# Six score buffers, ten activation items ahead of the gates, and four or five scatters per item by turns

## The chip, the cores and the metric

The kernel runs on one core of a Trainium2 chip. The metric is the device time of one execution in microseconds (us). The engines are named as in the profile: PE (matrix multiplications), PEld (its weight loads), DVE (vector), ACT (scalar), POOL (GpSimd), SP (the queue that issues most transfers). All engines run side by side, each through its own list of instructions in a fixed order.

## What is computed

One layer of a streaming encoder on 512 tokens (and 16 meta tokens) of width 2048: a mixer of 16 attention heads, then a channel mixer ("PEER") that picks 8 x 16 of 16384 single-neuron experts for each token. The change touches the second part only. Cut to that:

```
def block(hb):                                   # 128 tokens
    q = (hb @ w_query).reshape(128, 8, 2, 128)
    s = einsum('thpc,hpnc->thpn', q, sub_keys)   # 2 x 128 scores per head
    top_s, top_i = top_k(s, 16)
    cand_s = top_s[:, :, 0, :, None] + top_s[:, :, 1, None, :]
    cand_i = top_i[:, :, 0, :, None] * 128 + top_i[:, :, 1, None, :]
    best_s, best_j = top_k(cand_s, 16)           # over the 256 pairs of a head
    idx = take_along_axis(cand_i, best_j)
    g = softmax(best_s)
    a = gelu(einsum('thkd,td->thk', u[idx], hb))
    return einsum('thk,thkd->td', g * a, v[idx])
```

## The kernel before

The attention and the output projection fill the first 1030 us or so of the profile. The expert part has these stages.

**Queries and top-k.** For each of 16 query blocks (8 heads, two halves) `project` (line 199) multiplies a block of `w_q` with the tokens: 48 matmuls of 128x512, since each float32 product is made of three. A weight half arrives in `wr`; ACT casts quarters of it into `wh` (line 183), and DVE or POOL makes the remainder `wl` (line 184). `score` (lines 789 to 801) makes the scores of a block on PE into PSUM tile `zs`, and ACT copies them with a scale into `sc` (line 795), one of three buffers of [128, 4, 128] floats. After each second block `topk` (lines 737 to 787) puts some 70 instructions on DVE; the first reads and the match-and-replace steps of it use the two `sc` tiles of the head. The `sc` buffer of block c is free for block c+3 once line 750 of its head is done.

**Items.** The dense part treats tokens 128 to 511 against all experts in 128 chunks of 128 experts. Chunk j is an item: a block of `uT` is cut into `wh` and `wl`, 48 matmuls of 128x384 make its activations in PSUM tile `pa`, and ACT applies GELU into `ga` (line 873). For most items `ga` goes to DRAM (`a_scr`). The first `NAP` items after number `JC` (16) are made by `project` (line 212 on PE, `wl` on POOL); the others, called A(j), in the list `items` by `mm_u` (line 994 on PE, `wl` on DVE). Items 16 to 19 are of the first kind before, and A(20) is the first of the second; its `wl` too is made on POOL. At t = `GATES` = 1 of the list `gates` is called (lines 878 to 891): the exponential and the softmax over the chosen scores, the expert numbers `idx0`, and the scatter addresses `dst`. It needs the whole of `topk`. The list's DVE work is written out in order: the cut of A(21), then `gates`, then the cut of A(22).

**Work beside the items.** Two kinds of work are laid between the `wl` cuts of each A item after that. `due(WA)` hands out gathered rows for the first 128 tokens: `fetch` (line 828) is an indirect gather of 1 MB on POOL into one of three buffers `gr`, two rows ahead of `consume` (lines 843 and 846, two DVE instructions a row). It gives out 256 rows over A, D and V items. `scatter` (lines 910 to 932) has one step per call: line 914 sums the gates of one choice on DVE into one column of `tot`, and line 926 writes such a column into `g_scr` in DRAM, an indirect scatter of 128 single floats on POOL. There are 384 of each. `NSC` steps are given to each A or D item. PE, DVE, ACT and SP keep the order in which the list is written; POOL's order is chosen by the scheduler, which puts each scatter right behind its own sum rather than a head later.

**The rest.** After the A items come 16 D items, which read `g_scr` (`load_gates`, three items ahead), then eight rounds of V items, in which PE multiplies gated activations with rows of `v` (line 1016).

The order of the items is two lines, the first of which the change moves through `NAP`:

```
items = [("A", j) for j in range(JC + NAP, P)] + [("D", j) for j in range(JC)]
work = due(WA) + [sc] * NSC
```

Of the kernel before, what the change touches and what calls it, by code (L numbers as in the profile page):

```python
# [9 lines left out]
F32 = mybir.dt.float32  # L10
# [7 lines left out]
PSUM = bass.MemoryType.PSUM  # L18
DRAM = bass.MemoryType.DRAM

P = 128
# [3 lines left out]
D = 2048  # L25
KD = D // P
NH = 8
NTB = T // P
# [5 lines left out]
EPS = 1e-6  # L34
NEG = -1e30
H = D // 2
NAP = 4
GATES = 1
WA = 2.1
JC = 16  # L40
LEAD = JC // 2 + 1
NSC = 6
AHEAD = 3


class Lanes:
    """Steps of generators, run between pieces of the tensor engine's main stream.

    A generator yields (pieces to wait, next step uses the shared bank)."""

    def __init__(self):
        self.q = {}
# [39 lines left out]
def hymba_peer(ctx: ExitStack, tc: tile.TileContext, xT, w_in, w_fl, b_fg, g_mix, g_q, g_k, g_merge,  # L92
# [16 lines left out]

    nc.scalar.preload_act_table_set("natural_log_exp_and_others")  # L110

# [1 line left out]
    ident = cst.tile([P, P], F32, name="ident")  # L113
    make_identity(nc, ident)
    identb = cst.tile([P, P], BF16, name="identb")
# [101 lines left out]
    with ExitStack() as fctx:  # L217
        rawx = ExitStack()
        raw = rawx.enter_context(pool("raw", 16))

# [1 line left out]
        KV = [(0, 264), (264, 528)]  # L222
        QR = [(NM, S)]
        raws = [None] * 16

# [1 line left out]
        with ExitStack() as actx:  # L227
            at = actx.enter_context(pool("at", 2))
            qk = actx.enter_context(pool("qk", 1))
# [1 line left out]
            def t2(shape, dtype, name):  # L231
                return at.tile(shape, dtype, name=name, tag="t2", bufs=15)

            # the input, scaled by the gain; each projection is scaled by rstd as it leaves PSUM
            hh, hl = [], []
            flr = raw.tile([P, KD, NH], F32, name="flr", tag="raw")
            flh = raw.tile([P, KD, NH], F32R, name="flh", tag="raw")
# [2 lines left out]
            rstd = raw.tile([P, S], F32, name="rstd", tag="rstd", bufs=1)  # L240
# [48 lines left out]
            stx.close()  # L289
            mnx.enter_context(tc.manual_schedule(engines=ordered))  # L290

            # forget gate: cumulative log sigmoid, [head, token]
            fb_ = raw.tile([NH, S], F32, name="fb", tag="raw")
            for i, (lo, hi) in enumerate(KV):
                nc.vector.tensor_tensor(fb_[:, lo:hi], fps[i][:NH, :264], rstd[:NH, lo:hi], op=OP.mult)
# [55 lines left out]
            def pass3(ah, al, bh, bl):  # L351
                return ((ah, bh), (ah, bl), (al, bh))

            # -- stick-breaking head, keys on partitions --
            # (rows, width, [(key block, column offset, first query)])
            units = [(P, 512, [(2, 0, 256), (3, 256, 256)]), (P, 384, [(1, 0, 128)]),
                     (P, 512, [(0, 0, 0)]), (NM, 512, [(4, 0, 0)])]

            def sb_att(c, q, vh, vl):
# [26 lines left out]
                    sps[ui] = [(sh, sl, off, t0) for b, off, t0 in blks]  # L386
                    tops[ui] = a

                # sums over the key blocks so far, for the units before them
                def run_on(ui):  # L390
                    a, w = tops[ui], units[ui][1]
                    if ui == 0:
# [83 lines left out]
                lanes.add("misc", v_natural(c, ps, vh, vl), 1, True)  # L476
                lanes.add("att", sb_att(c, q, vh, vl), 1)

            # -- forgetting head, queries on partitions --
            def fox_norm(h, nm, ps, rng, gn, q):  # L480
                off = rng[0][0]
                xs = []
# [137 lines left out]
            lanes.drain()  # L620
        fcx.close()

# [1 line left out]
        pr = ctx.enter_context(pool("pr", 1, side="right"))  # L624
        hbn = pr.tile([P, D], F32, name="hbn")
        acc = pr.tile([P, D], F32, name="acc")
# [5 lines left out]
        with ExitStack() as mctx:  # L632
            mg = mctx.enter_context(pool("mg", 16))
            mt = mctx.enter_context(pool("mt", 2))
            mh, ml = [None] * KD, [None] * KD

            def merge(i):
                ps = psF.tile([P, 512], F32, name=f"pgs{i}", tag="o", bufs=1)
                nc.tensor.matmul(ps, ones, ssg[i], start=True, stop=True)
                rs = rsqrt(mt, ps, NH * P, [P, T], f"g{i}")  # L640
                for h in range(NH):
                    c = i * 8 + h
                    m = mt.tile([P, T], F32, name=f"mx{c}", tag="mx", bufs=2)
                    nc.vector.scalar_tensor_tensor(m, raws[c], gmer[:, c:c + 1], rs, op0=OP.mult, op1=OP.mult)
                    mh[c] = mg.tile([P, T], F32R, name=f"mh{c}", tag="mh")
                    ml[c] = raw.tile([P, T], F32R, name=f"ml{c}", tag="raw")
                    split(mh[c], ml[c], m)
                    yield 1, False

            lanes.add("mrg", merge(0), 0)  # L650
            for h in range(4, NH):
                gate(h, mt.tile([P, T], F32, name=f"ge{h}", tag="ge"))
            lanes.drain()
            for _ in merge(1):
                pass

# [1 line left out]
            ss2 = mt.tile([P, T], F32, name="ss2", bufs=1)  # L658

            def residual(c, ps):  # L660
                x = mt.tile([P, T], F32, name=f"xres{c}", tag="mx", bufs=2)
                nc.sync.dma_start(x, xT[:, c, NM:])
                r = mt.tile([P, T], F32, name=f"h2_{c}", tag="h2")
                nc.vector.tensor_tensor(r, ps[0], x, op=OP.add)
                hg = mt.tile([P, T], F32, name=f"hg{c}", tag="hg", bufs=1)
                nc.vector.tensor_scalar(hg, r, gffn[:, c:c + 1], None, op0=OP.mult)
                a = big.tile([P, T], F32R, name=f"bh{c}", tag="hh")
                b = big.tile([P, T], F32R, name=f"bl{c}", tag="hl")
                split(a, b, hg)
                bh.append(a)  # L670
                bl.append(b)
                if c == 0:
                    nc.gpsimd.tensor_tensor(ss2, r, r, op=OP.mult)
                else:
                    sq = mt.tile([P, T], F32, name=f"s2q{c}", tag="ge")
                    nc.gpsimd.tensor_tensor(sq, r, r, op=OP.mult)
                    nc.gpsimd.tensor_tensor(ss2, ss2, sq, op=OP.add)

                def g():
                    pm = pmisc(f"ph{c}")  # L680
                    for b in range(NTB):
                        nc.tensor.transpose(pm[:, b * P:b * P + P], r[:, b * P:b * P + P], ident)
                    hn = mt.tile([P, T], F32, name=f"hn{c}", tag="hn", bufs=1)
                    nc.scalar.copy(hn, pm)
                    nc.sync.dma_start(h_scr.rearrange("(b p) (c d) -> c p b d", p=P, d=P)[c],
                                      hn.rearrange("p (b d) -> p b d", d=P))
                    yield 1, True
                    pm = pmisc(f"phg{c}")
                    nc.tensor.transpose(pm[:, :P], hg[:, :P], ident)
                    nc.scalar.copy(hbn[:, c * P:c * P + P], pm[:, :P])  # L690
                lanes.add("misc", g(), 2 if c < 2 else 1, True)

            first = [project(w_out[c], mh, ml, [(0, T)], f"wo{c}", hfs=(0,)) for c in range(3)]
            for c in range(KD):
                ps = project(w_out[c], mh, ml, [(0, T)], f"wo{c}", ps=first[c] if c < 3 else None,
                             hfs=(1,) if c < 3 else (0, 1))
                residual(c, ps)
            q0p = project(w_q[0], bh, bl, [(0, T)], "wq0", hfs=(0,))
            lanes.drain()
            ssf = big.tile([P, T], F32, name="ssf", tag="ssf", bufs=1)  # L700
            nc.gpsimd.tensor_copy(ssf, ss2)

# [1 line left out]
        rawx.close()  # L704
        hbx = ExitStack()
        hbd = hbx.enter_context(pool("hbd", 1, side="right"))
# [5 lines left out]
        with ExitStack() as qctx:  # L712
# [76 lines left out]
            def score(c, qt, key, scs):  # L789
                z = psZ.tile([P, 512], F32, name=f"zs{c}", tag="z")  # L790
                for b in range(NTB):
                    nc.tensor.matmul(z[:, b * P:b * P + P], qt[:, b * P:b * P + P], key, start=True, stop=True)
                sc = qp.tile([P, NTB, P], F32, name=f"sc{c}", tag="sc", bufs=3)
                for b in range(NTB):
                    nc.scalar.activation(sc[:, b, :], z[:, b * P:b * P + P], AF.Copy, scale=rcol[:, b:b + 1])
                scs.append(sc)
                if len(scs) == 2:
                    topk(c // 2, scs)
                return
                yield  # L800
# [15 lines left out]

    bigx.close()

# [1 line left out]
    # (table, slot), the up rows of a head before its down rows  # L820
    order = [(x, h * TOPK + i) for h in range(PH) for x in range(2) for i in range(TOPK)]
    rows = {}

# [38 lines left out]
        done[0] = r.stop  # L862
        return [x for n in r for x in (consume(n),) * 2]

# [1 line left out]
    dn = ctx.enter_context(pool("dn", 2))  # L866
    gp = hbx.enter_context(pool("gp", 1, side="right"))
    ef = gp.tile([P, NTB, P], F32, name="ef")
# [34 lines left out]
    gt = ctx.enter_context(pool("gt", 3))  # L903
    pq = ctx.enter_context(pool("pq", 2))

    # the gates of the dense tokens, scattered head by head: an expert that several heads chose gets the
    # sum of its gates, written by each of them in turn with the heads so far
    g_flat = g_scr.rearrange("j i (t o) -> (j i t) o", o=1)

    def scatter():  # L910
# [20 lines left out]
                    head.append(w)  # L931
                yield

    # the tensor engine's order: A(j) makes the activations of experts i*P+j for all i, for later; D(j)
    # makes those of the first chunk, gated at once; R(j) fetches those made before and gates them;
    # V(j, half) adds their values to one half of the output's columns
    items = [("A", j) for j in range(JC + NAP, P)] + [("D", j) for j in range(JC)]
    for c in range(P // JC):
        for x in range(2 * JC):
# [106 lines left out]
    with tc.manual_schedule(engines=fixed):  # L1046
        sc = scatter()
        loaded = 0
        for t in range(len(items) + 1):
# [16 lines left out]
                gts = gates()  # L1066
            work = []
            if kind(t) in ("A", "D") and t > GATES:
                work = due(WA) + [sc] * NSC
            elif kind(t) == "V":  # L1070
                work = due(1, hold=items[t][1] % JC == JC - 1 and t < len(items) - JC)
            if nxt.get(t) is not None:
# [67 lines left out]
```

## Time and profile before

| | us |
|---|---|
| median of 3 runs | 3523.47 |
| lowest and highest of the runs | 3519.0 and 3527.59 |
| span of the profiled execution | 3525.9 |

| engine | busy us | share of the span | instructions |
|---|---|---|---|
| PE | 3398.5 | 96% | 17838 |
| DVE | 2402.1 | 68% | 4939 |
| ACT | 1296.8 | 37% | 2427 |
| POOL | 1096.4 | 31% | 916 |

These shares are means over stages with different limits, so the prediction reads them by stretches of the span: the windows view gives the busy time of each engine in a stretch, its count of instructions in brackets, the mean clock that PE was granted (1.00 is full) and the traffic. The count of PE instructions tells more than its busy time there, because the ends of matmuls are modelled: a matmul that runs at half clock is busy for twice as long.

### The profile page before, as it was taken

To read this page: it belongs to the slowest core of one execution; us is meant where nothing else is said; L and a number is where in the kernel's file an instruction comes from. 1 tells how busy PE (TensorE), PEld (TensorE's weight loads), DVE (VectorE), ACT (ScalarE), POOL (GpSimd) and SP (SyncE) were. 2 spreads that over 40 slices of the span, in tenths; PEclk is the share of its full clock that TensorE was granted. 3 is DMA by queue.
4 is the path that set the end of the run, shared out by engine and by line. 5 is a ranking of instruction groups with operands and counts; after the bars stand their busy time and mean duration, and the time that the engine had idled before them with its cause. 6 is when DMAs were issued, how large, how long until landed. Compare 5 with 4: busy or idle time off the path is not lost.

```text
span 3525.9 us, 49445 instructions
## 1 busy us (share of the span) xinstructions
PE 3398.5 (96%) x17838; PEld 2999.8 (85%) x17838; DVE 2402.1 (68%) x4939; ACT 1296.8 (37%) x2427; POOL 1096.4 (31%) x916
## 2 busy tenths in 40 slices
PE   8999999999999979789888999999999999999999
PEld 6888899988888779779877899999888888888887
DVE  7555666658449996556656666667777877877775
ACT  5444555444333323222222233333333333333332
POOL 2000000012238637767777611111122122112110
PEclk9999999999999989899888999999999999999999
DMA  3333333323442247667666777888888888888885
GB/s 122 126 105 106 107 106 104 107 87 110 141 132 91 89 147 241 219 204 250 220 205 217 246 287 285 288 292 287 319 305 314 300 313 311 308 310 312 312 306 169
DMA packets 224534, 749.23 MB, mean 212 GB/s; under 512 B 35360, under 2 KB 90784, under 8 KB 190880
## 3 DMA queue, kind: packets, MB, share of 16 engines
q1 hardware_dynamic: 168736, 452.23, 39.4%
q0 software_dynamic: 55552, 293.84, 23.0%
q8 instruction: 140, 2.29, 0.3%
q14 instruction: 106, 0.87, 0.1%
HBM read 690.19 MB, written 55.77 MB: 212 GB/s over the span
## 4 chain that ended last, share of the span: by engine, by line
PE 86%; DVE 8%; issue 3%; DMA 2%; POOL 0%; ACT 0%; SPq 0%; DVEq 0%; POOLq 0%; ACTq 0%
PE pv L1016 30%; PE pa L994 28%; PE pj_wo L212 5%; PE pj_sv L212 3%; PE pj_fv L212 3%; PE pj_sk L212 3%; PE pj_fk L212 3%; PE pj_fq L212 3%; PE pj_fg L212 3%; PE pj_sq L212 2%; DMA gr<-in_u_dram,idx 1%; DVE oh L783 1%; PE pj_wq L212 1%; DVE oh L779 1%; PE po L580 1%
## 5 line engine op out<-in xcount | busy, mean ns | idle before, releaser
L994 PE MATMUL pa<-dh,wl_A 128*128 128x384 f32 x1728 | 599.1, 347 | 46.9 <-DVE wl_A L184 23.3
L994 PE MATMUL pa<-dh,wh_A 128*128 128x384 f32 x1728 | 597.7, 346 | 25.9 <-issue 25.4
L994 PE MATMUL pa<-dl,wh_A 128*128 128x384 f32 x1728 | 598.1, 346 | 22.6 <-issue 22.1
L1016 PE MATMUL pv<-wh_V,pl 128*128 128x512 f32 x1536 | 597.5, 389 | 0.0
L1016 PE MATMUL pv<-wl_V,ph 128*128 128x512 f32 x1536 | 597.5, 389 | 0.0
L1016 PE MATMUL pv<-wh_V,ph 128*128 128x512 f32 x1536 | 597.5, 389 | 0.0
L184 DVE TENSOR_TENSOR wl_A<-wr_u,wh_A 128x512 fp32r<-128x512 f32 x428 | 294.4, 691 | 341.0 <-ACT wh_A L183 218.4
L183 ACT CAST wh_A<-wr_u 128x512 fp32r<-128x512 f32 x432 | 265.5, 620 | 656.2 <-PE pa L994 467.9
L183 ACT CAST wh_V<-wr_v 128x512 fp32r<-128x512 f32 x512 | 317.2, 621 | 507.1 <-PE pv L1016 504.8
L184 DVE TENSOR_TENSOR wl_V<-wr_v,wh_V 128x512 fp32r<-128x512 f32 x510 | 343.2, 689 | 221.7 <-ACT wh_V L183 221.5
L926 POOL DMA_INDIRECT g_scr<-tot,dst x384 | 429.3, 1118 | 149.5 <-issue 84.1
L994 PEld LDWEIGHTS pa<-dh,wl_A 128*128 128x128 f32 x1728 | 335.3, 194 | 61.2 <-issue 35.2
L828 POOL DMA_INDIRECT gr<-in_v_dram,idx x128 | 179.8, 1405 | 631.9 <-DVE acc L846 505.0
L994 PEld LDWEIGHTS pa<-dh,wh_A 128*128 128x128 f32 x1728 | 335.0, 194 | 37.3 <-issue 36.8
L994 PEld LDWEIGHTS pa<-dl,wh_A 128*128 128x128 f32 x1728 | 334.9, 194 | 36.2 <-issue 36.0
L828 POOL DMA_INDIRECT gr<-in_u_dram,idx x128 | 156.6, 1224 | 621.8 <-DVE gr L843 479.7
L1016 PEld LDWEIGHTS pv<-wh_V,ph 128*128 128x128 f32 x1536 | 288.3, 188 | 59.9
L1016 PEld LDWEIGHTS pv<-wl_V,ph 128*128 128x128 f32 x1536 | 288.3, 188 | 59.9
L1016 PEld LDWEIGHTS pv<-wh_V,pl 128*128 128x128 f32 x1536 | 288.3, 188 | 59.8
L843 DVE SCALAR_TENSOR_TENSOR gr<-gr,hbn 128x1024 f32<-128x1024 f32 x256 | 303.0, 1220 | 35.8 <-DMA gr<-in_u_dram,idx 31.1
L846 DVE SCALAR_TENSOR_TENSOR acc<-gr,coef,acc 128x1024 f32<-128x1024 f32 x256 | 318.1, 1284 | 2.0 <-DMA gr<-in_v_dram,idx 1.4
L348 POOL TENSOR_TENSOR osq<-o 128x512 f32<-128x512 f32 x14 | 14.5, 1036 | 525.6 <-ACT o L342 525.6
(388 smaller groups left out, 6197.0 us busy)
## 6 DMA issues: line engine op xcount, KB each, us to landing
wr_u<-in_uT_dram SPq DMA_DIRECT2D x256, 512.0 KB
wr_v<-in_v_dram SPq DMA_DIRECT2D x256, 512.0 KB
g_scr<-zero POOLq DMA_DIRECT2D x16, 1536.0 KB
gg<-g_scr SPq DMA_DIRECT2D x128, 192.0 KB
a_scr<-ga SPq DMA_DIRECT2D x112, 192.0 KB
gb<-a_scr SPq DMA_DIRECT2D x112, 192.0 KB
wr_wo<-in_w_out_dram SPq DMA_DIRECT2D x32, 512.0 KB
wr_wq<-in_w_q_dram SPq DMA_DIRECT2D x32, 512.0 KB
```

The lines of the kernel that those rows point to most:

```text
L183: nc.scalar.copy(hi, src)
L184: (lo_eng or nc.vector).tensor_tensor(lo, src, hi.bitcast(F32), op=OP.subtract)
L212: nc.tensor.matmul(ps[i][:, :hi - lo], wt[:, kk, :], ht[k][:, lo:hi], start=(k == 0 and n == 0), stop=(k == KD - 1 and n == 2))
L580: nc.tensor.matmul(po[:, t0:], vv, ww, start=f, stop=True, skip_group_check=not f)
L779: nc.vector.tensor_tensor(oh, abf[:, p].unsqueeze(2).to_broadcast([P, NTB * TOPK, TOPK]), iota16.unsqueeze(1).to_broadcast([P, NTB * TOPK, ...
L783: nc.vector.tensor_tensor(ohv, ohv, i1f[:, :, p, :].unsqueeze(2).to_broadcast([P, NTB, TOPK, TOPK]), op=OP.mult)
L828: nc.gpsimd.indirect_dma_start(out=r, out_offset=None, in_=(u, v)[x], in_offset=bass.IndirectOffsetOnAxis(ap=idx0[:, s:s + 1], axis=0))
L843: nc.vector.scalar_tensor_tensor(r[:, c], r[:, c], 1.0, hbn[:, c], op0=OP.mult, op1=OP.mult, accum_out=dots[:, y, h, i:i + 1])
L846: nc.vector.scalar_tensor_tensor(acc[:, c], r[:, c], coef[:, h, i:i + 1], acc[:, c], op0=OP.mult, op1=OP.add)
L926: w = nc.gpsimd.indirect_dma_start(out=g_flat, out_offset=bass.IndirectOffsetOnAxis(ap=dst[:, b, s:s + 1], axis=0), in_=tot[:, b, s:s + 1] ...
L994: nc.tensor.matmul(ps[:, :TD], wt[:, k % 4, :], ht[k], start=(k == 0 and n == 0), stop=(k == KD - 1 and n == 2))
L1016: nc.tensor.matmul(po["now"][n][b], a[:, bs], w_, start=(jj == 0 and pi == 0), stop=(jj == JC - 1 and pi == 2))
```

## The change

Three numbers are changed, and the choice of one of them by the parity of the item. The other lines of the diff only remove comments.

```diff
-NAP = 4
+NAP = 10
-NSC = 6
+NSC = (4, 5)
...
-                sc = qp.tile([P, NTB, P], F32, name=f"sc{c}", tag="sc", bufs=3)
+                sc = qp.tile([P, NTB, P], F32, name=f"sc{c}", tag="sc", bufs=6)
...
             if kind(t) in ("A", "D") and t > GATES:
-                work = due(WA) + [sc] * NSC
+                work = due(WA) + [sc] * NSC[t % 2]
```

In `due` the number of rows per item is worked out from `NAP` as well: an A item gets 2.1 x 256 / (0.975 x (2.1 x (128 - NAP - 2) + 256)) rows, 1.076 before and 1.104 now.

The first place is DVE's order at the end of the top-k, one piece of the difference. `res` is the last result of `topk` (line 786), `wl_A_21` and `wl_A_27` are the remainders of items 21 and 27, `es` the first step of `gates`.

```order
 L786 TENSOR_REDUCE res<-oh_12964 128x4x16
 L786 TENSOR_REDUCE res<-oh_12968 128x4x16
-L184 TENSOR_TENSOR wl_A_21_13286<-wr_u_21_13257,wh_A_21_13285 128x512
-L184 TENSOR_TENSOR wl_A_21_13290<-wr_u_21_13257,wh_A_21_13289 128x512
-L184 TENSOR_TENSOR wl_A_21_13294<-wr_u_21_13259,wh_A_21_13293 128x512
-L184 TENSOR_TENSOR wl_A_21_13298<-wr_u_21_13259,wh_A_21_13297 128x512
+L184 TENSOR_TENSOR wl_A_27_13718<-wr_u_27_13689,wh_A_27_13717 128x512
+L184 TENSOR_TENSOR wl_A_27_13722<-wr_u_27_13689,wh_A_27_13721 128x512
+L184 TENSOR_TENSOR wl_A_27_13726<-wr_u_27_13691,wh_A_27_13725 128x512
+L184 TENSOR_TENSOR wl_A_27_13730<-wr_u_27_13691,wh_A_27_13729 128x512
 L883 TENSOR_REDUCE es<-e 128x32
 L884 RECIPROCAL es<-es 128x32
```

The first item whose remainders stand behind the whole top-k on DVE is number 27 instead of 21; items 20 to 26 have theirs on POOL, and the gates stand behind item 27.

The second place is POOL's order where the gathers and scatters begin. `gr_4` and the like are gathered rows, `g_scr<-tot,dst` a scatter. Before:

```order
L828 DMA gr_3_13537<-in_u_dram,idx_8871 128x2048
L926 DMA g_scr<-tot,dst 6291456x1 x6
L828 DMA gr_4_13625<-in_u_dram,idx_8871 128x2048
L926 DMA g_scr<-tot,dst 6291456x1 x6
L828 DMA gr_5_13713<-in_u_dram,idx_8871 128x2048
L926 DMA g_scr<-tot,dst 6291456x1 x6
```

With the change:

```order
L828 DMA gr_3_13965<-in_u_dram,idx_8871 128x2048
L926 DMA g_scr<-tot,dst 6291456x1 x4
L828 DMA gr_4_14051<-in_u_dram,idx_8871 128x2048
L926 DMA g_scr<-tot,dst 6291456x1 x5
L828 DMA gr_5_14135<-in_u_dram,idx_8871 128x2048
L926 DMA g_scr<-tot,dst 6291456x1 x4
```

Between two gathers stand four or five scatters by turns instead of six. The 384 scatters take up 64 items before and 85.3 now.

## The prediction

> **What bounds the kernel now.** I read the page first, then the busy times by stretches, then who waited for whom in the two stretches that are not full.
>
> ```profile
> PE 3398.5 (96%) x17838; PEld 2999.8 (85%) x17838; DVE 2402.1 (68%) x4939; ACT 1296.8 (37%) x2427; POOL 1096.4 (31%) x916
> PE   8999999999999979789888999999999999999999
> POOL 2000000012238637767777611111122122112110
> ```
>
> The mean of 96% hides a hole in slices 14 to 23 of 40, and POOL, idle elsewhere, is at 6 to 7 tenths in most of those. The windows view, cut at the borders of the stages, has the amounts (busy us, instructions in brackets, then granted clock, DMA share and GB/s):
>
> ```profile
> 1050.00:1200.00 150.00, 150.00 (x704) 123.98 (x703) 139.51 (x518) 59.09 (x132) 125.03 (x97) 1.00 0.31 94
> 1200.00:1310.00 110.00, 84.35 (x418) 78.26 (x417) 107.67 (x387) 29.40 (x56) 41.98 (x29) 0.86 0.32 101
> 1310.00:2020.00 710.00, 628.67 (x3238) 590.40 (x3237) 444.32 (x1265) 194.10 (x341) 513.74 (x456) 0.91 0.70 227
> 2020.00:2340.00 320.00, 319.41 (x1842) 318.77 (x1841) 200.53 (x291) 109.93 (x194) 49.28 (x41) 1.00 0.80 287
> ```
>
> PE is full from 1050 to 1200 and from 2020 on (the slices have nines to the end). It is not from 1200 to 1310 (the end of the top-k, DVE at 98%) nor from 1310 to 2020 (the scatters, POOL at 72% by its records). Only these two can give anything, and the change touches both.
>
> **First hole: the end of the top-k.** PE's score matmuls and the first of item 16, from the timeline, then the waits of 1200 to 1310:
>
> ```profile
> 1195.76 1.05 PE L792 MATMUL zs<-key,qt 128*128 128x128 f32 x8
> 1207.76 1.05 PE L792 MATMUL zs<-key,qt 128*128 128x128 f32 x8
> 1222.93 2.08 PE L792 MATMUL zs<-key,qt 128*128 128x128 f32 x8 [3.02 <-ACT qt L811]
> 1236.43 1.05 PE L792 MATMUL zs<-key,qt 128*128 128x128 f32 x8
> 1237.24 0.42 PE L212 MATMUL pa<-dh,wh_u 128*128 128x384 f32 x1
> ```
> ```profile
> ACT sc L795 <- DVE i L750: 24.3, 2, 12.5
> PE pa L994 <- DVE wl_A L184: 13.5, 1, 13.5
> PE pa L212 <- ACT sc L795: 9.2, 1, 9.2
> ```
>
> A query block takes 12.0 us (1195.76 to 1207.76). Two steps later the scores should run at 1231.8, and they run at 1236.4: 4.7 lost. The cause is one step back: ACT stood 24.3 us in two waits for line 750, that is for a score buffer, with the weight casts queued behind it. The GELUs give the pitch of an item and the rest of the loss (items 16 to 127 and the 16 D items have one each; item 20's starts at 1287.32, item 21's at 1312.27):
>
> ```profile
> L873 ACT ACTIVATE ga<-pa x128: 478/485/495, 1253.1 to 2477.1; 128x384 f32<-128x384 f32 x128
> 1287.32 0.48 ACT L873 ACTIVATE ga<-pa 128x384 f32<-128x384 f32 x1
> 1312.27 0.49 ACT L873 ACTIVATE ga<-pa 128x384 f32<-128x384 f32 x1
> ...
> 2460.86 0.49 ACT L873 ACTIVATE ga<-pa 128x384 f32<-128x384 f32 x1
> 2469.18 0.48 ACT L873 ACTIVATE ga<-pa 128x384 f32<-128x384 f32 x1
> 2477.09 0.49 ACT L873 ACTIVATE ga<-pa 128x384 f32<-128x384 f32 x1 [3.66 <-PE pa L994]
> ```
>
> An undisturbed item takes 8.32 us (2460.86 to 2469.18). Items 16 to 20, begun at 1237.24, would end at 1278.9 and end at 1287.3: 8.4 lost. Item 21 takes 24.95 instead of 8.32: 16.6 lost, waiting for remainders that stand behind the whole top-k on DVE. Together 4.7 + 8.4 + 16.6 = **29.7 us**.
>
> What the change makes of it: with six buffers block c waits for block c-6, not c-3, so three more blocks (36 us of PE) lie between a score and the buffer that it needs, more than the longest wait of 12.5. PE then begins item 16 at 1232.6 and has eleven items whose remainders come from POOL: until 1232.6 + 91.5 = 1324.1. DVE's part:
>
> ```profile
> 1297.68 2.34 DVE L786 TENSOR_REDUCE res<-oh 128x64 f32<-128x1024 f32 x2
> 1299.94 2.49 DVE L184 TENSOR_TENSOR wl_A<-wr_u,wh_A 128x512 fp32r<-128x512 f32 x4
> 1302.34 0.68 DVE L883 TENSOR_REDUCE es<-e 128x32 f32<-128x512 f32 x1
> 1305.77 0.68 DVE L184 TENSOR_TENSOR wl_A<-wr_u,wh_A 128x512 fp32r<-128x512 f32 x1
> ```
>
> The top-k, which is DVE's own work without gaps, ends at 1299.9 as before, 24 us ahead of need. The two edits need each other: buffers alone would bring PE to item 21 13 us sooner, to wait 13 us longer. The gates (1302.34 to 1305.77, 3.4 us) now stand behind item 27's cuts, which follow the casts and so PE; they are hidden by the 8.3 us of item 27, and cost up to 3.4 if that cover fails. I cost them at nothing. The six more items on POOL cost this:
>
> ```profile
> L184 POOL TENSOR_TENSOR wl_u<-wr_u,wh_u 128x512 fp32r<-128x512 f32 x16 | 25.4, 1602 | 23.7 <-ACT wh_u L183 23.7
> ```
>
> Four cuts of 1.60 are 6.4 us of an item's 8.32, so POOL keeps up; it would hold PE only above 2.08 a cut. The hole goes: **-29.7**.
>
> **Second hole: the scatters.** From item 21's GELU to the last are 122 items in 1164.8 us; at 8.32 they are 1015.0. So **149.8 us** are lost. The count of matmuls says where: 3238 between 1310 and 2020 where 710 us have room for 4096 (48 per 8.32); the missing 858 are 148.7 us. POOL in that stage, and in a stretch of it (1585 to 1655) in which PE ran at full pace:
>
> ```profile
> L926 POOL DMA_INDIRECT g_scr<-tot,dst x384 | 429.3, 1118 | 149.5 <-issue 84.1 <-DVE junk L914 37.3 <-DVE wl_A L184 17.9
> L828 POOL DMA_INDIRECT gr<-in_u_dram,idx x40 | 49.3, 1231 | 31.9 <-DVE gr L843 13.6 <-issue 8.8 <-DMA gr<-in_u_dram,idx 8.3
> L828 POOL DMA_INDIRECT gr<-in_v_dram,idx x32 | 35.2, 1100 | 15.1 <-issue 7.9 <-DVE acc L846 5.9 <-DVE junk L914 0.6
> ```
> ```profile
> L926 POOL DMA_INDIRECT g_scr<-tot,dst x39 | 44.7, 1146 | 11.9 <-issue 7.6 <-DVE wl_A L184 1.8 <-DVE junk L914 1.2
> L828 POOL DMA_INDIRECT gr<-in_u_dram,idx x5 | 7.0, 1390 | 1.5 <-issue 1.2 <-DVE wl_A L184 0.3
> L828 POOL DMA_INDIRECT gr<-in_v_dram,idx x3 | 4.2, 1387 | 0.9 <-issue 0.9
> ```
>
> Every POOL transfer has 0.30 us before it that no record fills (the last fence below), so 456 of them cost 513.8 + 136.8 = 651 of the 710 us: POOL is the bound, whatever its busy share says. With that gap a scatter costs 1.42 and a gather 1.47 on the average. An item needed 6 x 1.42 + 1.076 x 1.47 = 10.1 us of POOL against 8.32 of PE; over 64 items that is 646 against 532. POOL falls behind, the gathers in the same queue come late, and then everything drags until POOL has caught up (four windows of 10 us in the columns of above, and POOL's timeline):
>
> ```profile
> 1670.00:1680.00 10.00, 7.40 (x20) 4.98 (x20) 2.98 (x5) 1.13 (x2) 7.87 (x8) 0.64 0.48 166
> 1680.00:1690.00 10.00, 6.09 (x14) 3.32 (x12) 2.35 (x9) 0.73 (x2) 7.56 (x9) 0.50 0.45 158
> 1690.00:1700.00 10.00, 5.44 (x15) 4.56 (x16) 2.19 (x9) 2.03 (x4) 4.47 (x5) 0.50 0.37 111
> 1700.00:1710.00 10.00, 10.00 (x59) 10.00 (x59) 9.86 (x30) 3.60 (x6) 7.87 (x7) 1.00 0.82 271
> ```
> ```profile
> 1693.47 0.97 POOL L926 DMA_INDIRECT g_scr<-tot,dst  x1 [0.30 <-issue]
> 1699.06 0.97 POOL L926 DMA_INDIRECT g_scr<-tot,dst  x1 [4.61 <-DVE junk L914]
> ```
>
> PE goes from 15 matmuls in 10 us to 59 in the ten that follow POOL's idle 4.61 us. What holds PE within such a patch the waits of 1310 to 2020 don't name; most of its idle time there has no releaser:
>
> ```profile
> PE pa L994 <- issue: 70.3, 101, 3.0
> ```
>
> That a patch ends when POOL's backlog is gone can be seen.
>
> With the change an item has 4.5 scatters and 1.104 gathers. By the stage's means that is 4.5 x 1.42 + 1.104 x 1.47 = 8.0 us; by the full-pace stretch, 4.5 x 1.45 + 1.104 x 1.69 = 8.37. These are the two ends, and the pace of PE, 8.32, lies between them. I take 8.37, since full pace would now be the rule (in that stretch POOL got through 47 transfers in 8.4 items, 5.6 an item, which is just what the change asks for). The backlog then grows by 0.05 us an item, 4 us in 85.3 items, where it grew by 1.8 an item. The three dragging rows above have 49 matmuls where three full ones have 177: 128 of them at 0.173 us are 22 us for a patch. I allow the 4 us and two thirds of one patch, 14: **18 us** stay. By the lower end it is 0, by the upper one see rival (2).
>
> DVE has room: 444 of 710 us, and its sums per item become fewer. The scatters end some 21 items later than before, 87 items into the list, and the gates of the D items are read from the 99th on, so SP doesn't stand at that read; were POOL 12 items late it would.
>
> **The sum** against the profiled execution: 3525.9 - 29.7 - 149.8 + 18 = 3364.4. The median of the runs is 2.4 under that span, so **3362 us**.
>
> **Rivals.** (1) The patches belong to the scatters themselves and not to POOL's lag: 384 scatters stay, 149.8 stays, only 29.7 goes, 3496.2 and 3494 as a median. For it speaks that the 70.3 us above show no engine as the one waited for. Against it speak 70 us at full pace from 1585 to 1655 with POOL just as busy, and the end of the patch with POOL's idling. [...] Chance 0.08.
>
> (2) POOL stays slower than PE, because its transfers take longer beside a busy DVE. A scatter took 0.97 us at 1693, while DVE stood, and 1.146 in the full-pace stretch. At the worst each of an item's four cuts on DVE (0.68 us each, above) holds a transfer up for its whole length: 5.6 x 1.27 + 2.7 = 9.8 us, and 85.3 x 1.5 = 128 us stay. Half of that, 64, gives 3346.4 + 64 = 3410, as a median 3408. Against it speaks that the full-pace stretch has all four cuts in it and still 8.37. Chance 0.17, with 0.04 of it near the worst. [...]
>
> (3) Slower than before: patches come by time whenever POOL has no pause, and at 8.37 against 8.32 it has none. They cost 149.8 / 64 = 2.34 us an item, and there are 85.3 such items instead of 64: 199.7. The sum is 3525.9 - 29.7 + 49.9 = 3546, as a median 3544. It decides at POOL's 8.32 us an item; against it speaks that a patch ended at once when the backlog did. Chance 0.04.
>
> (4) The first hole stays, because something else than `sc` holds ACT (the two PSUM banks of `zs`, or `qt`), so the change doesn't do what it says there: 3364.4 + 29.7 = 3394, as a median 3392. Only the score buffers stand in the waits above. Chance 0.06.
>
> (5) Nothing of the second hole stays: 3525.9 - 179.5 = 3346.4, as a median 3344. Chance 0.20.
>
> **How the numbers follow.** My forecast has 0.45. The range of 3341 to 3425 takes in (2), (4) and (5) and leaves out (1), (3) and the worst of (2), 0.16. A measurement tells about 0.2% (7 us) from no change here, as the three runs lie within 0.25%. Faster has all but (3) and a little for what I overlooked: 0.94; within 0.2% 0.02; slower 0.04.
>
> **What would show it.** PE at 418 matmuls between 1200 and 1310 should be at some 600, with no wait of ACT's score copy for line 750. The GELU of item 27 should come near 1333. From there the GELUs should keep 8.32 through item 113, with POOL in single pauses of over 0.30 and PE's granted clock at 1.00. DVE should stand idle between the end of the top-k near 1300 and the gates near 1325. I am wrong if patches with the clock at 0.5 come back at the same number per item, or if PE waits for POOL's cuts in items 20 to 26.

## The result and the profile after

| | before | after |
|---|---|---|
| median of 4 runs, us | 3522.45 | 3398.96 |
| lowest to highest | 3519.0 to 3527.59 | 3395.77 to 3403.36 |
| span of the profiled execution, us | 3525.9 | 3394.1 |

The change makes the kernel faster: ratio 0.9652, 95% interval 0.9639 to 0.9666. It gains 123.5 us where 160 were forecast; 3399 lies inside the range, 37 us above the number.

The page of after, its busy times and the slices of PE and POOL:

```profile
PE 3349.5 (99%) x17838; PEld 2978.1 (88%) x17838; DVE 2382.6 (70%) x4915; ACT 1297.5 (38%) x2427; POOL 1159.0 (34%) x940
PE   8999999999999999999989999999999999999999
POOL 2000000003226865777776775111112121112120
```

PE's hole is down to one slice with an 8, while POOL still stands at 5 to 8 tenths for 13 slices. The windows of after at the same borders as before, from 1200 on:

```profile
1200.00:1310.00 110.00, 110.00 (x609) 105.25 (x608) 105.08 (x365) 40.06 (x74) 72.68 (x49) 1.00 0.44 141
1310.00:2020.00 710.00, 690.48 (x3864) 680.48 (x3863) 496.80 (x1302) 233.12 (x409) 512.34 (x433) 0.97 0.80 270
2020.00:2340.00 320.00, 315.44 (x1787) 311.93 (x1786) 217.78 (x363) 112.98 (x202) 96.64 (x82) 0.98 0.83 288
```

From 1200 to 1310 PE has 609 matmuls instead of 418: nothing is left of the first hole. From 1310 to 2020 it has 3864 where 4096 have room, so 232 x 0.1733 = 40 us are still lost there, and some more behind 2020. The GELUs of items 26 and 27 and of the last item, in ACT's timeline of after:

```profile
1319.91 0.48 ACT L873 ACTIVATE ga<-pa 128x384 f32<-128x384 f32 x1
1329.59 0.49 ACT L873 ACTIVATE ga<-pa 128x384 f32<-128x384 f32 x1
...
2344.06 0.49 ACT L873 ACTIVATE ga<-pa 128x384 f32<-128x384 f32 x1 [3.66 <-PE pa L994]
```

They split the gain. Item 26 has its GELU 32.6 us sooner than before, where ACT's timeline has it at 1352.47:

```profile
1352.47 0.48 ACT L873 ACTIVATE ga<-pa 128x384 f32<-128x384 f32 x1
```

From there to the last are 117 items, 973.4 us at full pace: 1124.6 before, so 151.2 lost, and 1024.2 now, so **50.7 lost**. What follows the last GELU is 1050.0 instead of 1048.8. Together 32.6 + 100.5 - 1.2 = 131.9, the difference of the spans. "Lost" below is always this count, from item 26's GELU to the last.

POOL by groups, 1340 to 2080 (count, busy us and mean ns, then the idle time ahead of the group and its releasers):

```profile
L926 POOL DMA_INDIRECT g_scr<-tot,dst x374 | 441.8, 1181 | 140.6 <-issue 95.1 <-DVE junk L914 21.4 <-DVE wl_A L184 10.7
L828 POOL DMA_INDIRECT gr<-in_v_dram,idx x47 | 54.2, 1152 | 31.4 <-DVE acc L846 10.7 <-issue 10.3 <-DVE junk L914 8.9
L828 POOL DMA_INDIRECT gr<-in_u_dram,idx x44 | 53.5, 1216 | 18.8 <-issue 9.1 <-DVE gr L843 6.1 <-DVE junk L914 1.5
```

The six sums are 740.3, the whole window. Of the 190.8 idle, 465 x 0.30 = 139.5 are the gap ahead of every transfer. So a transfer costs (549.5 + 139.5) / 465 = 1.48 and an item of 5.604 transfers 8.30 us, between the two ends forecast (8.0 and 8.37) and just at PE's 8.32. The other 51.3 us POOL stood. Item for item the kernel had what it needed, and still 50.7 us went.

By the gaps between the starts of matmuls they went in four patches, near 1465, 1753, 1894 and 2073 (12.0, 16.3, 9.2 and 8.8 us), and two of some 1.5 us near 1564 and 2031. The first one, in windows of 1 us (PE's busy time, in brackets every matmul that touches the window, then clock, DMA share, GB/s):

```profile
1464.00:1465.00 1.00, 1.00 (x7) 1.00 0.82 311
1465.00:1466.00 1.00, 0.63 (x3) 1.00 0.65 222
1466.00:1467.00 1.00, 0.54 (x3) 1.00 0.20 74
...
1468.00:1469.00 1.00, 0.01 (x1) 0.86 0.25 82
1469.00:1470.00 1.00, 0.48 (x1) 0.50 0.99 246
...
1483.00:1484.00 1.00, 1.00 (x8) 1.00 0.92 336
```

Counted by their starts, PE has five or six matmuls a microsecond until 1465 and two in each of the next two, while it still has full clock; the clock follows at 1469 (0.50) and is back at 1483 (1.00), after PE has run densely for some 5 us. So the clock is a follower here, not the cause. In the dense stretch at half clock, from 1477 to 1482, PE's timeline has a matmul every 0.32 us instead of every 0.173, with records of 0.52 us instead of 0.34: 1.85 and 1.5 times as long, where the section on the time before says twice. The spacing makes 2.5 us of this patch's 12.0, so most of it is the thin stretch ahead. The DMA engines are mostly idle where that begins (share 0.20 at 1466) and full three microseconds later (0.99 at 1469), so their load does not go with it here, and the waits of 1310 to 2340 name no engine:

```profile
PE pa L994 <- issue: 23.5, 36, 1.6
```

### The profile page after: what moved, and what is told of

Same layout as the page of the kernel before. It is cut to its first block, busy times and chain, and to the rows that moved or that the text cites. A ratio compares the mean times of both kernels' runs of the same rounds, so it can differ in the third digit from the quotient of the medians.

```text
span 3394.1 us, 49431 instructions
## 1 busy us (share of the span) xinstructions
PE 3349.5 (99%) x17838; PEld 2978.1 (88%) x17838; DVE 2382.6 (70%) x4915; ACT 1297.5 (38%) x2427; POOL 1159.0 (34%) x940
## 4 chain that ended last, share of the span: by engine, by line
PE 97%; DVE 2%; issue 1%; DMA 0%; ACT 0%; SPq 0%; DVEq 0%; ACTq 0%
PE pv L1016 30%; PE pa L994 30%; PE pj_wo L212 5%; PE pj_wq L212 5%; PE pj_sv L212 3%; PE pj_fv L212 3%; PE pj_sk L212 3%; PE pj_fk L212 3%; PE pj_fq L212 3%; PE pj_fg L212 3%; PE pa L212 2%; PE pj_sq L212 2%; PE po L580 1%; PE po L436 1%; PE z L370 1%
## 5 line engine op out<-in xcount | busy, mean ns | idle before, releaser
L994 PE MATMUL pa<-dh,wl_A 128*128 128x384 f32 x1632 | 555.8, 341 | 9.9 <-issue 9.6
L994 PE MATMUL pa<-dl,wh_A 128*128 128x384 f32 x1632 | 555.5, 340 | 7.3 <-issue 7.1
L994 PE MATMUL pa<-dh,wh_A 128*128 128x384 f32 x1632 | 555.4, 340 | 7.0 <-issue 6.8
L926 POOL DMA_INDIRECT g_scr<-tot,dst x384 | 452.8, 1179 | 143.7 <-issue 97.2
L184 DVE TENSOR_TENSOR wl_A<-wr_u,wh_A 128x512 fp32r<-128x512 f32 x404 | 278.6, 691 | 263.0 <-ACT wh_A L183 168.1
L183 ACT CAST wh_A<-wr_u 128x512 fp32r<-128x512 f32 x408 | 249.9, 620 | 507.1 <-PE pa L994 367.0
L828 POOL DMA_INDIRECT gr<-in_v_dram,idx x128 | 187.1, 1462 | 531.7 <-DVE acc L846 409.4
L994 PEld LDWEIGHTS pa<-dh,wl_A 128*128 128x128 f32 x1632 | 310.7, 190 | 13.8 <-issue 13.4
L994 PEld LDWEIGHTS pa<-dh,wh_A 128*128 128x128 f32 x1632 | 311.2, 191 | 12.5 <-issue 12.0
L994 PEld LDWEIGHTS pa<-dl,wh_A 128*128 128x128 f32 x1632 | 311.0, 191 | 11.4 <-issue 10.9
```

Of the source, the lines that this page charges most:

```text
L183: nc.scalar.copy(hi, src)
L184: (lo_eng or nc.vector).tensor_tensor(lo, src, hi.bitcast(F32), op=OP.subtract)
L828: nc.gpsimd.indirect_dma_start(out=r, out_offset=None, in_=(u, v)[x], in_offset=bass.IndirectOffsetOnAxis(ap=idx0[:, s:s + 1], axis=0))
L926: w = nc.gpsimd.indirect_dma_start(out=g_flat, out_offset=bass.IndirectOffsetOnAxis(ap=dst[:, b, s:s + 1], axis=0), in_=tot[:, b, s:s + 1] ...
L994: nc.tensor.matmul(ps[:, :TD], wt[:, k % 4, :], ht[k], start=(k == 0 and n == 0), stop=(k == KD - 1 and n == 2))
```

## The experiments

The kernels are called `e1` to `e12`. They ran in three groups, each with 13 runs of the kernel before beside it, whose medians are 3524.44 us (`e1` to `e4`), 3496.72 (`e5` to `e8`) and 3540.73 (`e9` to `e12`). The first two groups ran on one chip (14), the third on another (3). The kernel before thus differs by 44 us between groups, so a time is compared with runs of its own group, and where that can't be done the text says so.

### The parts of the change

Score buffers alone (`e3`):

```diff
-                sc = qp.tile([P, NTB, P], F32, name=f"sc{c}", tag="sc", bufs=3)
+                sc = qp.tile([P, NTB, P], F32, name=f"sc{c}", tag="sc", bufs=6)
```

> Six score buffers alone. Nothing is left out. Theory A (PE comes 13 us sooner to item 21 and waits 13 us longer there for the top-k on DVE): 3523, no change beyond 5 us. Rival B (the score waits are a loss of their own): 13 us less, 3510.

3526.95 us, ratio 1.0008 (0.9989 to 1.0027). Item 20's GELU comes at 1270.3 instead of 1287.3, and item 21's at 1312.8 instead of 1312.3: what the buffers give, the wait behind the top-k takes.

Ten items ahead alone (`e9`):

```diff
-NAP = 4
+NAP = 10
```

> The kernel before with ten items ahead and nothing else (three score buffers, six scatters). If the first hole is the sum of two causes (13.1 us behind score buffers, 16.6 us behind the top-k), the 16.6 us at item 21 go and the 13.1 us stay: 16.6 us under before, ratio 0.995. If the items bring something only together with the buffers: ratio 1.000. The loss in the scatter stage stays near 150 us in both.

3526.74 us, ratio 0.9967 (0.9951 to 0.9983), which holds the 0.995 expected and leaves out 1.000. ACT's timeline has items 20 and 21:

```profile
1286.46 0.48 ACT L873 ACTIVATE ga<-pa 128x384 f32<-128x384 f32 x1
1294.78 0.48 ACT L873 ACTIVATE ga<-pa 128x384 f32<-128x384 f32 x1
```

Item 21 is at full pace and item 20 as late as before; the scatter stage loses 164.5 us, somewhat more than the 150 expected. So the first hole is a sum: the items give their 16.6 us alone, and only the buffers need the other edit.

Both, with six scatters (`e1`):

```diff
-NSC = (4, 5)
+NSC = (6, 6)
```

> Ten items ahead and six score buffers as in the change, but six scatters per item as before. Nothing is left out of the computation. Theory A (the two edits remove the hole at the end of the top-k and nothing else): about 30 us under before, 3493, with the patches of the scatter stage as before (about 150 us lost there). Rival B (the scatters of the change also owe their gain to the later start): clearly lower than 3480.

3494.39 us, ratio 0.9906 (0.9881 to 0.993): 30.1 us under before. 152.0 lost in the scatter stage, as before the change.

Four and five scatters, the rest as before (`e2`):

```diff
-NAP = 10
+NAP = 4
...
-                sc = qp.tile([P, NTB, P], F32, name=f"sc{c}", tag="sc", bufs=6)
+                sc = qp.tile([P, NTB, P], F32, name=f"sc{c}", tag="sc", bufs=3)
```

> Four and five scatters per item by turns alone, with four items ahead and three score buffers as before. Nothing is left out. Theory A (the scatter edit alone takes about 99 of the 150 us lost in the scatter stage): 3523 - 99 = 3424. Rival B (it needs the other edits): above 3460.

3419.17 us, ratio 0.9697 (0.9673 to 0.972): 105.3 under before. 44.2 lost, and item 21 waits as before:

```profile
1285.78 0.49 ACT L873 ACTIVATE ga<-pa 128x384 f32<-128x384 f32 x1
1310.56 0.49 ACT L873 ACTIVATE ga<-pa 128x384 f32<-128x384 f32 x1
```

So the gain is 30 for the first hole and some 100 for the second, each where the prediction had it. What is too large is the rest in the second.

### Room on POOL

Four scatters at every item (`e4`); so that the 384 end in time for the D items, a step sums and scatters the same choice:

```diff
-NSC = (4, 5)
+NSC = (4, 4)
...
-        for h in range(PH + 1):
+        for h in range(PH):
...
-                if h < PH:
-                    total(h, b, i)
-                if h > 0:
-                    s = (h - 1) * TOPK + i
+                total(h, b, i)
+                if True:
+                    s = h * TOPK + i
```

> The change, with four scatters per item instead of four and a half (a step sums and scatters the same choice, so that the 384 steps still end before the gates are read). Nothing is left out. POOL then needs 4 x 1.48 + 1.104 x 1.48 = 7.6 us an item instead of 8.3, against PE's 8.32. Theory A (patches come of POOL's lag): the 51 us still lost in the scatter stage fall to 15 or less, 3363. Theory B (each scatter costs PE time wherever it stands): the same 384 scatters, 3399.

3345.29 us, ratio 0.9497 (0.9465 to 0.9529): the fastest version that computes everything, 179 us under the kernel before in this group and, by the two ratios, some 1.6% under the change. Windows and POOL's groups of 1340 to 2080:

```profile
1310.00:2020.00 710.00, 710.00 (x4098) 710.00 (x4097) 515.87 (x1296) 249.68 (x433) 508.82 (x425) 1.00 0.85 289
```
```profile
L925 POOL DMA_INDIRECT g_scr<-tot,dst x355 | 430.5, 1213 | 122.3 <-issue 81.1 <-DVE wl_A L184 19.8 <-DVE junk L914 10.8
L828 POOL DMA_INDIRECT gr<-in_u_dram,idx x51 | 56.8, 1114 | 30.3 <-DVE gr L843 13.6 <-issue 7.3 <-DVE acc L846 6.0
L828 POOL DMA_INDIRECT gr<-in_v_dram,idx x48 | 53.4, 1111 | 47.5 <-DVE acc L846 35.9 <-issue 7.8 <-DVE coef L851 1.7
```

PE is full, nothing is lost (-0.4). A transfer costs (540.7 + 136.2) / 454 = 1.49, an item of 5.104 of them 7.6 us, 0.7 under PE's pace. All 384 scatters are still there, beside a DMA share of 0.85: scatters alone make no patch in this group.

Five scatters (`e8`):

```diff
-NSC = (4, 5)
+NSC = (5, 5)
```

> The changed kernel with five scatters at every item. Lag theory: POOL needs 5 x 1.51 + 1.09 x 1.41 = 9.1 us an item, 0.77 over PE's 8.32, for 76.8 items: 59 us, and up to the 51 us that the changed kernel loses at a need of just 8.36 on top: 3405 to 3460 us with 60 to 110 us lost in the stage. Rival (the loss of the changed kernel, 0.6 us per item with scatters, is the price of any full stage): 46 us, 3394 us.

3411.05 us, ratio 0.9745 (0.9723 to 0.9768), 65.4 lost. By its own groups a transfer costs 1.47, an item of 6.104 of them 9.0, and 0.67 x 76.8 = 51 us follow from that alone. The price per item of the rival, 46, is too low. With `e1`, by the same count, there is a series:

| kernel | POOL's need, us an item | items with scatters | lost by the need alone | lost |
|---|---|---|---|---|
| `e4`, four | 7.6 | 96 | 0 | 0 |
| after, four and five | 8.30 | 85.3 | 0 | 51 |
| `e8`, five | 9.0 | 76.8 | 51 | 65 |
| `e1`, six | 10.2 | 64 | 123 | 152 |

After and `e1` lose 51 and 29 us over the need's own amount. `e8` ran in another group, loses 14 over it, and loses it by another wait. PE's waits of 1340 to 2080 name DVE's cuts, and nothing is listed without a releaser:

```profile
PE pa L994 <- DVE wl_A L184: 42.4, 16, 5.4
```

POOL loaded without transfers, on the kernel with four scatters (`e5`):

```diff
+    pad = gp.tile([P, P], F32, name="pad")
...
                     head.append(w)
+                    for _ in range(2):
+                        nc.gpsimd.memset(pad, 0.0)
```

> This is the kernel with four scatters per item, in which nothing of the scatter stage was lost, with two POOL fills of 128x128 (0.204 us each) behind every scatter: POOL gets 1.6 to 2.4 us more per item and not one transfer more, and its transfers stand further apart than there. Lag theory (patches come because POOL is behind its items): POOL needs 9.2 to 10.0 us an item against 8.32, so 84 to 160 us are lost over 96 items, 3430 to 3505 us, with patches. Rival (patches come where POOL's transfers follow each other without a pause, whatever its lag): none come, 3345 us.

3517.36 us, ratio 1.0053 (1.0036 to 1.0069), above both. It went partly wrong: POOL's order is the scheduler's, and as the fills read nothing it put some ahead of the cuts of the first items, where the first of them waited for the memory of the top-k. The waits of 1250 to 1300:

```profile
POOL pad L933 <- DVE res L786: 44.0, 1, 44.0
...
PE pa L212 <- POOL wl_u L184: 40.1, 1, 40.1
```

That puts item 26 at 1392.2, 72 us late, outside the stage. For the same reason the fills were used up at 1812, and so one trace holds both cases. First the fills in one stretch (busy us and count, clock, DMA share, GB/s), then PE, PEld, DVE, ACT and POOL with and without fills:

```profile
1600.00:1700.00 100.00, 24.70 (x120) 0.90 0.69 225
```
```profile
1600.00:1700.00 100.00, 83.81 (x442) 82.03 (x441) 54.52 (x128) 26.04 (x45) 76.94 (x169) 0.90 0.69 225
1700.00:1800.00 100.00, 81.11 (x414) 79.32 (x413) 55.03 (x145) 25.16 (x44) 76.23 (x167) 0.89 0.66 217
1840.00:1940.00 100.00, 100.00 (x579) 100.00 (x578) 70.65 (x172) 34.39 (x62) 74.56 (x66) 1.00 0.88 293
1940.00:2040.00 100.00, 100.00 (x579) 100.00 (x578) 76.91 (x190) 35.20 (x61) 73.19 (x61) 1.00 0.86 290
```

With fills PE has 442 and 414 matmuls in 100 us, at 169 - 120 = 49 transfers and, with 120 fills again, 47; without them 579, at 66 and 61 transfers and more traffic. So what costs PE time here is POOL's time being used up, and not the number of its transfers. That comparison lies within one execution. But the loss is not of the kind of after's patches, since its waits have names (1410 to 1840):

```profile
PE pa L996 <- DVE wl_A L184: 66.5, 19, 6.7
DVE gr L843 <- DMA gr<-in_u_dram,idx: 81.6, 16, 9.2
DVE acc L846 <- DMA gr<-in_v_dram,idx: 66.2, 12, 8.0
```

The rows come late, DVE stands for 147.8 us, its cuts come late, and PE waits for them. Nothing is listed for PE without a releaser. Whether a used-up POOL brings after's patches as well is not shown by this run.

### Where the 51 us come from

The trace of after offers two places at which POOL stands though it is behind: the first scatter of a head (1.4 to 5.2 us at seven of them), which in the program has to wait for those of the head before, and gathers that wait for a row buffer (10.7 and 6.1 us behind lines 846 and 843, by POOL's groups above). Theory: these waits build the lag, and the lag makes the gathers late, DVE stand and its cuts late.

Head waits away (`e10`):

```diff
-        for h in range(PH + 1):
-            head = []
+        head = []
+        for h in range(PH + 1):
+            last, head = head, []
...
-                    for x in head:
+                    for _, x in head + [y for y in last if y[0] != b]:
...
-                    head.append(w)
+                    head.append((b, w))
```

> The changed kernel; a scatter waits only for those of the head before that belong to its own token block (others write other addresses), and these have long landed. Transfers, sizes, order and result stay. Lag theory: as with two targets, POOL no longer stands at head changes, 25 us of its 51 us of standing go, and the stage loses 5 to 20 us instead of 51: 3345 to 3365 us. Rival (the gain with two targets came from the second scratch tensor, as other addresses in DRAM): 51 us stay, 3395 to 3400 us.

The changed kernel in the same group (`e12`):

> The changed kernel once more, beside the others of this call and the same runs of the kernel before: 3390 to 3405 us, 45 to 55 us lost in the scatter stage. If the time is nearer 3370, part of what the four rows and the two targets gained is a difference between days.

3392.54 us (3390.53 to 3395.01) against 3404.86 (3400.43 to 3409.44); ratios to before 0.9587 (0.9559 to 0.9616) and 0.9623 (0.9593 to 0.9653). POOL's timeline at the first change of head, in the changed kernel and then without the wait:

```profile
1429.61 0.97 POOL L926 DMA_INDIRECT g_scr<-tot,dst  x1 [0.30 <-issue]
1435.09 0.97 POOL L926 DMA_INDIRECT g_scr<-tot,dst  x1 [4.50 <-DVE junk L914]
```
```profile
1430.21 0.97 POOL L927 DMA_INDIRECT g_scr<-tot,dst  x1 [0.31 <-issue]
1431.48 0.97 POOL L927 DMA_INDIRECT g_scr<-tot,dst  x1 [0.30 <-issue]
```

The waits are gone, but 48.6 us are lost against 59.4. The changed kernel lost a little more than expected. Without the head waits 5 to 20 were expected: this part of the theory falls. The head waits are worth some 11 us, and patches come without them.

A fourth row buffer (`e6`; the edits that make room for it are left out):

```diff
-            fetch(1)
-        fetch(n + 2)
+            fetch(1)
+            fetch(2)
+        fetch(n + 3)
...
-    gt = ctx.enter_context(pool("gt", 3))
+    gt = ctx.enter_context(pool("gt", 4))
```

> The changed kernel with a fourth row buffer, each gather issued one consumption (some 7.5 us) sooner; to make room the gates of later stages are read two items later and from two buffers, and rows are gated one item later (LEAD). POOL's work, its scatters and its lag stay. If a lagging POOL harms PE through gathers that come late to DVE (which then stands with the remainder cuts of PE behind it), the lags of 10 to 18 us become harmless and the 51 us of the scatter stage go: 3345 to 3360 us. If lag harms PE in another way, or the patches are the transfers' own, the stage loses 40 to 60 us as before: 3390 to 3410 us. The smaller buffers behind may cost some us in the last stages; so the verdict is read from the GELUs of the scatter stage.

3364.19 us, ratio 0.9618 (0.9591 to 0.9644); 19.0 lost. That looks like the late rows, but DVE's waits for rows (us, times, longest) say the opposite. After, then four rows, then five scatters:

```profile
DVE acc L846 <- DMA gr<-in_v_dram,idx: 5.5, 2, 3.7
DVE gr L843 <- DMA gr<-in_u_dram,idx: 1.2, 3, 0.5
```
```profile
DVE acc L847 <- DMA gr<-in_v_dram,idx: 24.8, 10, 6.7
DVE gr L844 <- DMA gr<-in_u_dram,idx: 20.8, 9, 4.7
```
```profile
DVE acc L846 <- DMA gr<-in_v_dram,idx: 76.1, 22, 7.7
DVE gr L843 <- DMA gr<-in_u_dram,idx: 72.9, 23, 7.1
```

DVE stands 6.7 us for rows where 50.7 are lost, 45.6 where 19.0 are, and 149.0 where 65.4 are. Late rows are not what makes the patches of after. In `e6` and `e8` they are the wait that shows: PE waits 10.2 and 42.4 us for cuts, which DVE makes behind those rows, and no idle time of PE is listed without a releaser. Nor is the gain of `e6` clear of the group: its ratio, 0.9618, is that of the changed kernel in `e12`, 0.9623.

Later rows, on the kernel with four scatters (`e11`):

```diff
-            fetch(1)
-        fetch(n + 2)
+            pass
+        fetch(n + 1)
```

> The kernel with four scatters per item (nothing lost), each gather issued one consumption (7.7 us) later. The transfers have a median of 11.6 us between landing and use there; 3.9 us would be left, and below zero in many cases, while POOL has room. Theory that lag harms PE through late rows alone: DVE stands some 2 to 5 us at one row in three, its cuts with it, and 20 us or more are lost: 3365 us or more. Theory that what harms is POOL's time being used up, with late rows as one sign of it: under 10 us, 3345 to 3355 us.

3349.28 us, ratio 0.947 (0.9441 to 0.9498), 2.0 lost. It tells nothing of late rows: in its trace every gather stands behind the same number of scatters as in `e4`, since the scheduler places POOL's instructions and not the order in which they are written. It counts as `e4` once more, in another group, with the same outcome.

Two scatter targets (`e7`):

```diff
+    g_odd = scr.tile([P, P, TD], F32, name="g_odd")
...
-    g_flat = g_scr.rearrange("j i (t o) -> (j i t) o", o=1)
+    g_flat = [g.rearrange("j i (t o) -> (j i t) o", o=1) for g in (g_scr, g_odd)]
...
-                        out=g_flat, out_offset=bass.IndirectOffsetOnAxis(ap=dst[:, b, s:s + 1], axis=0),
+                        out=g_flat[(h - 1) % 2], out_offset=bass.IndirectOffsetOnAxis(ap=dst[:, b, s:s + 1], axis=0),
```

> The changed kernel with the scatters of every second head written to a second scratch tensor that nobody reads (their gates are left out of the result). The first scatter of a head then no longer waits for the last ones of the head before. All transfers, their sizes and their number stay. Lag theory: the seven waits of 1.4 to 5.2 us at head changes (25 us of POOL in a stage of 700) go, POOL catches up between, and the 51 us lost shrink to 25 or less: 3350 to 3375 us. Rival (patches belong to the density of transfers): 51 us stay or grow, 3395 to 3410 us.

This version leaves the gates of every second head out of the result. 3344.91 us (3344.0 to 3350.79), ratio 0.9557 (0.9536 to 0.9578); 6.7 lost. Windows of two targets and of no head wait:

```profile
1310.00:2020.00 710.00, 709.35 (x4088) 708.39 (x4087) 527.93 (x1376) 246.43 (x432) 545.39 (x464) 1.00 0.86 288
```
```profile
1310.00:2020.00 710.00, 690.20 (x3868) 678.14 (x3867) 496.22 (x1301) 231.31 (x407) 519.12 (x437) 0.98 0.81 271
```

464 transfers at (545.39 / 464 + 0.30) = 1.48 us, the price of after, 8.3 us an item, and PE is full. So a need as large as PE's pace does not by itself cost 51 us. Why two targets do without patches is **open**: it is not the head waits (`e10` has none either, and the same list of transfers on POOL). It may be the second tensor, or the group, in which the kernel before took 44 us less than beside `e10`; the changed kernel did not run in that group. The same caution holds for the four rows.

The traces speak for the group. Idle time of PE before a matmul that no wait names, from 1340 to 2120 of each trace, is 70.3 us before the change and 23.5 after, 65.1, 18.6 and 61.3 in `e1` to `e3`, and 83.0, 19.6 and 26.2 in `e9`, `e10` and `e12`. In `e5` to `e8` none is listed, though POOL has less room in `e5` and `e8` than in after. In `e4` and `e11`, where POOL has room, it is none and 1.1, in groups whose other kernels have it. So these stops came where two things met: POOL without room, and something in which the second group differs from the others. What that is stays open; it is not the chip alone, since the first group ran on the same one.

## Why the prediction was right, and where not

**The bounds** held. Only the two holes gave something, and the parts alone gave 30 and 105 us.

**The first hole.** 29.7 forecast, 32.6 by item 26's GELU and 30.1 by `e1`. No wait of the score copies is left, item 27 came at 1329.6 (near 1333 forecast), and the gates are hidden behind it. "The two edits need each other" was right of the buffers (0 alone) and wrong of the items, which gave some 14 us alone (3540.73 to 3526.74); the sum does not use it.

**The second hole.** That POOL is the bound through its 0.30 us gap was right: 7.6 us an item lose nothing, 9.0 and 10.2 lose more than their difference to 8.32, and loading POOL without transfers costs PE 24 and 29 us of 100 (`e5`). The need, 8.0 to 8.37 by the two prices, came out at 8.30.

**The step that failed** is the residual: "The backlog then grows by 0.05 us an item, 4 us in 85.3 items", and "two thirds of one patch, 14". It was 50.7 us, nearly all in four patches of 9 to 16, where 18 were forecast, 32.7 too few. The rate was right; what was wrong is that a queue with no room was priced by the mean growth of its backlog alone. 11 of them are head waits, which the prediction did not look for (`e10` against `e12`, in a group where 59.4 were lost); the rest are patches whose own cause stays open, as the prediction said of what holds PE within one. They are missing in the second group, where `e7` (which has no head waits) and `e6`, at the need of after, lose 6.7 and 19.0; so how far 18 falls short depends on the group too, though the changed kernel itself did not run there. The other differences are -2.9 for the first hole, 1.2 behind the items, -1.4 because the loss before is 149.8 from item 21 and 151.2 from item 26, and 7.3 that do not belong to the mechanism: the median of after stands 4.9 above its span, where 2.4 below was taken over from before.

**The rivals.** (1) Patches that belong to the scatters: no, 384 of them without one in `e4`. (2) POOL slower beside DVE: a scatter took 1.181 on the average against 0.97 alone, and the need stayed under 8.32. Who starts first decides it in the trace of after. DVE's and POOL's timelines of after:

```profile
1819.09 2.48 DVE L846 SCALAR_TENSOR_TENSOR acc<-gr,coef,acc 128x1024 f32<-128x1024 f32 x2
1824.09 0.69 DVE L184 TENSOR_TENSOR wl_A<-wr_u,wh_A 128x512 fp32r<-128x512 f32 x1
```
```profile
1820.52 1.89 POOL L926 DMA_INDIRECT g_scr<-tot,dst  x1 [5.20 <-issue]
1824.00 0.97 POOL L926 DMA_INDIRECT g_scr<-tot,dst  x1 [0.30 <-DMA g_scr<-tot,dst]
```

The scatter of 1820.52 began while row instructions ran, which ended at 1821.57, and it ended 0.84 us after them. The scatter of 1824.00 began ahead of the cut and took 0.97. Of the 373 scatters between 1340 and 2080, 341 end within 0.04 us of that rule: 0.97 us after their start, or 0.84 after the end of the DVE instruction that had been running for at least 0.03 us, whichever is later. What was too much in the prediction is its "worst", that each cut holds a transfer up for its whole length: a transfer that starts first, as that of 1824.00, is not held. At 3408 the rival came near in time by another cause. (3) Patches by time whenever POOL has no pause: not at 2.34 us an item (after has 0.6), but its condition, no pause at 8.32, was the right place to look. (4), the nearest in time with 3392, fell with item 26. (5) nothing stays: reached by 3345.29 with four scatters, one step further than the change.

## What to carry to other kernels

Where one in-order engine feeds a full one, give it room: at a need of 100% of the pace 51 us were lost though the mean fitted (6.7 in `e7`, in the second group), and at 92% none. Before costing a hole at a mean rate, look for the waits inside the feeder's own list. And where the scheduler orders an engine, read the order that came out: two experiments here (the fills, the later rows) did not do on POOL what their code says.

## What was not expected of the hardware

- Within the first patch of after PE starts two to four matmuls a microsecond and then one or none, against nearly 6, with no wait that the profile names; it begins at full clock, with a DMA share of 0.20. POOL meanwhile goes through its transfers at its quickest (0.97 us and 0.30), and stands when its backlog is gone, as in after's POOL timeline:

```profile
1473.64 0.97 POOL L926 DMA_INDIRECT g_scr<-tot,dst  x1 [0.30 <-issue]
1482.30 1.02 POOL L828 DMA_INDIRECT gr<-in_v_dram,idx  x1 [7.69 <-DVE junk L914]
```

- The same kernel before took 3497, 3524 and 3541 us in three groups of 13 runs, each within 22 us, and the first two on the same chip. The kernel with four scatters, which has no patches, took 3345 and 3349 (`e4`, `e11`) in groups where the kernel before differs by 16. Where it differs was not tried.
